# Dealing the last channel block's sums and the meta rows over the token blocks of an output projection

## The chip, the core and the metric

The kernel runs on one core of one Trainium2 chip. The metric is device time in microseconds (us) of the execution, lower is better. Three runs of the kernel before took 1312.33, 1314.13 and 1315.68 us; their median, 1314.13 us, stands for the kernel. The core's engines work side by side, each through its own queue in order: TensorE (PE, matmuls and transposes, with its weight loads as PEld), VectorE (DVE), ScalarE (ACT), GpSimd (POOL) and SyncE (SP), which issues the DMAs.

## The reference

One decoder layer over 1024 tokens of width 1024, with 16 learned meta rows put ahead of them. Cut to what matters here:

```python
a = rmsnorm(h, ln_mix_pre)                       # h: 16 meta rows, then 1024 tokens
proj = a @ w_in
y_diff = diff_attention(...)                     # 512 channels
y_hgrn = hgrn2(...)                              # 512 channels
mix = concatenate([y_diff, y_hgrn], -1) @ w_out  # the output projection, 1024 x 1024
h = h + rmsnorm(mix, ln_mix_post)
a = rmsnorm(h, ln_ffn_pre)
y = conv_ffn(a, ...)                             # 1024 -> 5632, causal convolution of width 3, -> 1024
h = h + rmsnorm(y, ln_ffn_post)
return h[N_META:]
```

The meta rows are dropped at the end, but the convolution looks two rows back, so the last two of them go through the output projection and the norms as well.

## The kernel before

All products are taken in three matmuls of 32-bit operands: each operand is split into a high part and a low part (names ending in `h` and `l`), and high x high, high x low and low x high are added in PSUM.

Tokens are cut into blocks 1 to 8 of 128 rows; "block 0" is the two meta rows. The eight channel blocks k = 0 to 7 of the mixed heads (128 channels each) are stored to DRAM (`msc`) and loaded again per token block: tile `mp` holds channels 0 to 6 or 0 to 7 of a token block, loaded in two halves, and `m7` holds channel block 7 of all eight token blocks. The output projection has two halves of 512 output columns. The first half ran beside the last head; the result of channel blocks 0 to 6 lies in `y0`. Channel block 7 was not ready then, so its product is still to be added: `out_last(p)` does that for token block p. It is three matmuls into a bank `pz`, an addition into `y0` on VectorE, a squared sum on ScalarE (tile `jz`, sums in `ssy`), a small scaling, and for p < 3 the multiplication with the gain on GpSimd (`y0_gain`); later blocks get their gain at the head of their own turn.

The change lies in the loop over i = 1 to 8 of the second half. A turn of it:

- issues the DMAs for the next block: `second_load` (two halves of `mp`, lines L1041) and `load_xh` (the residual rows, L1189);
- runs `run` = `out_part` for k = 0 to 3 into bank `py`, 12 matmuls (lines L1012, L1014, L1016), then `trans(i - 2)`, eight transposes (L1230) of the normalised rows `a` of an earlier block, then k = 4 to 7, 12 more;
- calls `post(i)`: squared sum of the second half on ScalarE (`junk`), `tmp` = sum x gain on VectorE, the reciprocal root from two small ScalarE steps, two VectorE steps that add both halves to the residual `xh`, its store to DRAM (`hsc`, L1210), then the second norm: a square over 1024 columns on ScalarE, two small steps, and the VectorE step that writes `a`.

After `trans` ScalarE copies the transposed rows into `at`. When enough blocks are there, `t_split` casts a quarter of `at` to its high part on ScalarE (`t`) and VectorE takes the low part; the feed-forward matmuls (`pq`) start from them. `meta_part` computes the second half of block 0 with 17 matmuls (L1025 and three of `out_part`), which `post(0)` takes up.

TensorE's order is written out by hand in the program (it is the order of the calls). The other engines' queues are ordered by a scheduler that weighs costs of its own, so a call that is moved also moves rows on VectorE, ScalarE, GpSimd and SyncE. Nearly all their instructions carry line L53, a helper; they are told apart by tile names. The eight PSUM banks (`ps_b`) go round in the order of the calls. The tiles of `mp` share three places: block 2's place was block 7's of the first half, block 4's was block 1's.

The weights `wo` of the second half are loaded and split while the first half ends; the low part of the last of them (`wol`, k = 7) is made on VectorE.

Of the kernel before, what the change touches and what calls it, by code (L numbers as in the profile page):

```python
# [22 lines left out]
KD = D // P  # L23
# [62 lines left out]
def layer_kernel(ctx: ExitStack, tc: tile.TileContext, x, meta, table, lbl, gpre, gpost, win,  # L86
# [76 lines left out]
    def rstd_of(dst, ss, n):  # L163
        A.activation(dst, ss, AF.Ln, bias=eps[: dst.shape[0]], scale=1.0 / n)
        A.activation(dst, dst, AF.Exp, scale=-0.5)
# [3 lines left out]
    def long_tile(name):  # L169
        return mxp.tile([P, 8, WN[0]], F32, tag="X0", name=name).rearrange("p a c -> p (a c)")  # L170
# [833 lines left out]
    def tok(i):  # L1004
        return (2, 14) if i == 0 else (P, start(i))

    def out_part(m, py, wo, ks, first, last):
        r = m.shape[-1]
        for k in ks:
            hi, lo = wo[k]  # L1010
            mh, ml = m[:, 0, k], m[:, 1, k]
            T.matmul(py[:r], mh, hi, start=(first and k == ks[0]), stop=False)  # L1012
            yield 216
            T.matmul(py[:r], mh, lo, start=False, stop=False)  # L1014
            yield 216
            T.matmul(py[:r], ml, hi, start=False, stop=(last and k == ks[-1]))  # L1016
            yield 216
# [42 lines left out]
    def y0_gain(p):  # L1060
        r = tok(p)[0]
        return G.tensor_tensor(y0[:r, p], y0[:r, p], gpo0[:r], op=ALU.mult)

    def out_last(p):
        r = tok(p)[0]
        py = ps_b(f"pz{p}")
        m = m0_7 if p == 0 else k7(p)
        for _ in out_part(m, py, wo0[KD - 1:], range(1), True, True):
            pass
        V.tensor_tensor(y0[:r, p], y0[:r, p], py[:r], op=ALU.add)  # L1070
        junk = qp.tile([P, 512], F32, tag="junk", name=f"jz{p}", bufs=1)
        A.activation(junk[:r], y0[:r, p], AF.Square, accum_out=ssy[:r, p, 0:1])
        A.activation(ssy[:r, p, 0:1], ssy[:r, p, 0:1], AF.Identity, bias=eps[:r], scale=1.0 / D)
        if p < 3:
            y0_gain(p)
# [27 lines left out]
    def ps_b(name):  # L1103
        return pp.tile([P, 512], F32, tag="b", name=name)
# [65 lines left out]
    wo = load_wo(1)  # L1170
# [20 lines left out]
    def post(i, py, free=None):  # L1191
        r, t0 = tok(i)
        xh = xhs.pop(i)
        if i % 2:
            a2 = long_tile(f"a2_{i}")[:, :D]
        elif i == 0:
            a2 = xh
        else:
            a2 = bp.tile([P, D], F32, tag="a2", name=f"a2_{i}", bufs=1)
        tmp = qp.tile([P, 512], F32, tag="tmp", name=f"tmp{i}", bufs=1)  # L1200
        junk = qp.tile([P, 512], F32, tag="junk", name=f"junk{i}", bufs=1)
        s1, s2 = ssy[:r, i, 1:2], ssy[:r, i, 2:3]
        A.activation(junk[:r], py[:r], AF.Square, accum_out=s1)
        V.tensor_tensor(tmp[:r], py[:r], gpo[:r], op=ALU.mult)
        A.activation(s1, s1, AF.Ln, bias=ssy[:r, i, 0:1], scale=1.0 / D)
        A.activation(s1, s1, AF.Exp, scale=-0.5)
        V.scalar_tensor_tensor(xh[:r, :512], y0[:r, i], s1, xh[:r, :512], ALU.mult, ALU.add)
        V.scalar_tensor_tensor(xh[:r, 512:], tmp[:r], s1, xh[:r, 512:], ALU.mult, ALU.add)
        if i:
            SY.dma_start(hsc[P * (i - 1): P * i, :], xh)  # L1210
        if i:
            A.activation(a2[:r], xh[:r], AF.Square, accum_out=s2)
        else:
            s3 = ssy[:r, i, 3:4]
            for half, s_ in ((0, s2), (1, s3)):
                A.activation(free[:r], xh[:r, 512 * half:512 * half + 512], AF.Square, accum_out=s_)
            V.tensor_tensor(s2, s2, s3, op=ALU.add)
        rstd_of(s2, s2, D)
        V.scalar_tensor_tensor(a2[:r], xh[:r], s2, gfb[:r], ALU.mult, ALU.mult)
        a2t[i] = a2  # L1220

    def trans(i):
        r, t0 = tok(i)
        a2 = a2t.pop(i)
        cs = slice(t0 - 14, t0 - 14 + r)
        for half in range(2):
            pt = ps_b(f"pa2_{i}_{half}")
            for j in range(4):
                k = 4 * half + j
                T.transpose(pt[:, j * r:(j + 1) * r], a2[:r, P * k: P * (k + 1)], ident[:r, :r])  # L1230
            pv = pt[:, : 4 * r].rearrange("p (k t) -> p k t", k=4)
            ks = slice(4 * half, 4 * half + 4)
            for p in range(2):
                lo_, hi_ = max(cs.start, C0[p]), min(cs.stop, C0[p] + 2 * WN[p])
                if lo_ < hi_:
                    A.copy(
                        at2[p][:, ks, lo_ - C0[p]:hi_ - C0[p]], pv[:, :, lo_ - cs.start:hi_ - cs.start])
# [32 lines left out]
    def run(*args):  # L1270
        for _ in out_part(*args):
            pass

    def k7(i):
        return m7[:, i - 1:i].rearrange("p b l t -> p l b t")

    for i in range(1, NBLK):
        py = ps_b(f"py1_{i}")
        if i >= 3:
            y0_gain(i)  # L1280
        if i == 1:
            load_xh(1)
            load_xh(0)
        if i + 1 < NBLK:
            second_load(i + 1)
            load_xh(i + 1)
        run(blocks[i], py, wo, range(4), True, False)
        if i == 3:
            trans(1)
        if i > 3:  # L1290
            trans(i - 2)
        if i == 5:
            trans(0)
        run(blocks[i], py, wo, range(4, 7 if i == 1 else 8), False, i > 1)
        if i == 1:
            pm = ps_b("py1_0")
            for _ in meta_part(pm, wo, True):
                pass
            for p in range(3):
                out_last(p)  # L1300
            run(k7(1), py, wo[KD - 1:], range(1), False, True)
            post(1, py)
            ysum = xhs.pop("sum")
            for l in range(2):
                A.copy(ysum[:2, 512 * l:512 * l + 512], pm[32 * l:32 * l + 2])
            G.tensor_tensor(ysum[:2, :512], ysum[:2, :512], ysum[:2, 512:], op=ALU.add)
            for p in (3, 4):
                out_last(p)
            continue
        post(i, py)  # L1310
        if i == 2:
            post(0, ysum[:, :512], ysum[:, 512:])
        if i == 5:
            t_split(0, 0, quarter(0, 0), ep, "e0")
            t_split(0, 4, quarter(0, 4), ep, "e1")
        if i == 7:
            t_split(0, 7, quarter(0, 7), mxp, "X2", WN[0])
            t_split(0, 6, quarter(0, 6), mxp, "X1", WN[0])
        if i in (2, 3):
            for p in (1 + 2 * i, 2 + 2 * i):  # L1320
                out_last(p)
    close(q_cm, ml_cm, y_cm, wo_cm, ws_cm)

    xu_cm, xup = pool("xu", 2)
# [363 lines left out]
```

## Time and profile before

| | |
|---|---|
| median of 3 runs | 1314.13 us (1312.33 to 1315.68) |
| profiled execution, its own time | 1315.74 us |
| its span, first to last instruction | 1313.9 us |
| mean granted TensorE clock | 0.996 |
| TensorE busy | 1283.4 us, 98% |
| VectorE busy | 887.4 us, 68% |
| ScalarE busy | 697.6 us, 53% |
| GpSimd busy | 482.0 us, 37% |

Times in the rows are counted from the span's start. The stage of the change lies between about 556 us (the first matmuls of block 1's second half) and 645 us. A row of the timeline is: start, duration, engine, line, operation, out<-in, shapes, count, and in brackets the idle time of the engine before it and what ended that. In a table of stretches a row is: stretch, its length, busy time and count of PE, PEld, DVE, ACT and POOL, then the granted clock, the busy share of the DMA engines and GB/s. A row of waits is: who waited, for whom, us in total, times, the longest. Matmuls overlap, so the pace is read from starts, not from durations.

### The profile page before, as it was taken

To read this page: it belongs to the slowest core of one execution; us is meant where nothing else is said; L and a number is where in the kernel's file an instruction comes from. 1 tells how busy PE (TensorE), PEld (TensorE's weight loads), DVE (VectorE), ACT (ScalarE), POOL (GpSimd) and SP (SyncE) were. 2 spreads that over 40 slices of the span, in tenths; PEclk is the share of its full clock that TensorE was granted. 3 is DMA by queue.
4 is the path that set the end of the run, shared out by engine and by line. 5 is a ranking of instruction groups with operands and counts; after the bars stand their busy time and mean duration, and the time that the engine had idled before them with its cause. 6 is when DMAs were issued, how large, how long until landed. Compare 5 with 4: busy or idle time off the path is not lost.

```text
span 1313.9 us, 26100 instructions
## 1 busy us (share of the span) xinstructions
PE 1283.4 (98%) x10154; PEld 1188.1 (90%) x10154; DVE 887.4 (68%) x1488; ACT 697.6 (53%) x1639; POOL 482.0 (37%) x387
## 2 busy tenths in 40 slices
PE   8999999999999999999999999999999999999997
PEld 7999999899989998777999999999999997888875
DVE  7574646465645574547897877877778768697586
ACT  8565466547644763456754544444544445464553
POOL 5231423232313310353066566576666631010121
PEclk9999999999999999998999999999999999999999
DMA  6243655273643533687222222222222138854263
GB/s 212 93 102 84 126 113 113 66 149 84 115 120 67 121 109 108 227 274 252 87 73 78 85 75 79 86 76 81 76 79 88 57 104 282 310 194 162 87 209 120
DMA packets 116418, 165.04 MB, mean 126 GB/s; under 512 B 10099, under 2 KB 57523, under 8 KB 116294
## 3 DMA queue, kind: packets, MB, share of 16 engines
q1 hardware_dynamic: 93062, 151.84, 34.9%
q0 software_dynamic: 23232, 11.54, 7.5%
q8 instruction: 80, 1.31, 0.4%
q14 instruction: 44, 0.36, 0.1%
HBM read 134.24 MB, written 52.17 MB: 142 GB/s over the span
## 4 chain that ended last, share of the span: by engine, by line
PE 49%; DVE 4%; ACT 2%; issue 1%; DVEq 0%; ACTq 0%
PE pd L1537 5%; PE pd L1538 5%; PE pd L1536 5%; PE pb L1378 4%; PE pb L1380 4%; PE pb L1379 4%; PE pa L1378 3%; PE pa L1380 3%; PE pa L1379 3%; PE pc L1380 3%; PE pc L1378 3%; PE pc L1379 3%; DVE t L53 1%; DVE c L53 1%; PE py L1012 1%
## 5 line engine op out<-in xcount | busy, mean ns | idle before, releaser
L1378 PE MATMUL pb<-t,uh 128*128 128x258 f32 x504 | 142.4, 283 | 2.3 <-DVE u L53 2.3
L1379 PE MATMUL pb<-t,uh 128*128 128x258 f32 x504 | 141.8, 281 | 0.0
L1380 PE MATMUL pb<-t,ul 128*128 128x258 f32 x504 | 141.8, 281 | 0.0
L1537 PE MATMUL pd<-wl,gh 128*128 128x512 f32 x308 | 122.0, 396 | 1.2 <-DVE wl L53 1.1
L1536 PE MATMUL pd<-wh,gh 128*128 128x512 f32 x308 | 121.7, 395 | 0.0
L1538 PE MATMUL pd<-wh,gl 128*128 128x512 f32 x308 | 121.6, 395 | 0.0
L53 DVE SCALAR_TENSOR_TENSOR c<-uu,cwt,c 128x514 f32<-128x514 f32 (+1 forms) x88 | 96.9, 1101 | 20.0 <-ACT c L53 19.3
L53 POOL TENSOR_TENSOR c<-c,c 128x514 f32<-128x514 f32 (+1 forms) x44 | 63.8, 1450 | 122.5 <-ACT c L53 119.1
L1378 PEld LDWEIGHTS pb<-t,uh 128*128 128x128 f32 x504 | 95.0, 189 | 2.7 <-DVE u L53 2.7
L1380 PEld LDWEIGHTS pb<-t,ul 128*128 128x128 f32 x504 | 95.1, 189 | 0.0
L1378 PE MATMUL pa<-t,uh 128*128 128x258 f32 (+1 forms) x336 | 95.1, 283 | 0.0
L1379 PEld LDWEIGHTS pb<-t,uh 128*128 128x128 f32 x504 | 95.1, 189 | 0.0
L1380 PE MATMUL pc<-t,ul 128*128 128x258 f32 (+1 forms) x336 | 95.0, 283 | 0.0
L1380 PE MATMUL pa<-t,ul 128*128 128x258 f32 (+1 forms) x336 | 94.9, 282 | 0.0
L1378 PE MATMUL pc<-t,uh 128*128 128x258 f32 (+1 forms) x336 | 94.7, 282 | 0.0
L1379 PE MATMUL pa<-t,uh 128*128 128x258 f32 (+1 forms) x336 | 94.6, 282 | 0.0
L1379 PE MATMUL pc<-t,uh 128*128 128x258 f32 (+1 forms) x336 | 94.5, 281 | 0.0
L53 DVE SCALAR_TENSOR_TENSOR c<-ug,cwt,c 128x514 f32<-128x514 f32 (+1 forms) x88 | 88.3, 1005 | 1.3 <-ACT c L53 0.6
L53 ACT CAST uh<-ra 128x512 fp32r<-128x512 f32 x67 | 41.2, 618 | 62.9 <-PE pb L1379 41.4
L53 POOL TENSOR_TENSOR ul<-ws,uh 128x512 fp32r<-128x512 f32 x42 | 59.1, 1408 | 39.3 <-ACT uh L53 39.3
L1537 PEld LDWEIGHTS pd<-wl,gh 128*128 128x128 f32 x308 | 57.7, 187 | 16.6 <-DVE wl L53 2.6
L53 DVE TENSOR_TENSOR ul<-ra,uh 128x512 fp32r<-128x512 f32 x42 | 39.8, 947 | 48.5 <-ACT uh L53 48.5
(388 smaller groups left out, 4176.3 us busy)
## 6 DMA issues: line engine op xcount, KB each, us to landing
ra<-in_wup_dram SPq DMA_DIRECT2D x88, 256.0 KB, 2.7
mp<-msc SPq DMA_DIRECT2D x23, 512.0 KB, 5.5
tsc<-in_wdown_dram SPq DMA_DIRECT2D x44, 256.0 KB, 4.4
wi<-tsc SPq DMA_DIRECT2D x44, 256.0 KB, 2.8
gi<-gsc SPq DMA_DIRECT2D x33, 256.0 KB, 4.7
wi<-in_wdown_dram SPq DMA_DIRECT2D x33, 256.0 KB, 5.2
gsc<-c SPq DMA_DIRECT2D x22, 257.0 KB, 2.1
tsc<-in_wdown_dram POOLq DMA_DIRECT2D x22, 256.0 KB, 7.4
```

The costliest lines, as they stand in the source:

```text
L53: ins = call(*args, **kw)
L1012: T.matmul(py[:r], mh, hi, start=(first and k == ks[0]), stop=False)
L1378: T.matmul(pt, hi[:, s], th[:, k], start=(first and k == 0), stop=False, skip_group_check=True)
L1379: T.matmul(pt, hi[:, s], tl[:, k], start=False, stop=False, skip_group_check=True)
L1380: T.matmul(pt, lo[:, s], th[:, k], start=False, stop=(k == 3), skip_group_check=True)
L1536: T.matmul(py, gh[:, s], wh, start=(k == 0 and pr not in (3, 7)), stop=False, skip_group_check=True)
L1537: T.matmul(py, gh[:, s], wl, start=False, stop=False, skip_group_check=True)
L1538: T.matmul(py, gl[:, s], wh, start=False, stop=(k == NH - 1), skip_group_check=True)
```

## The change

Three things are put elsewhere; nothing is computed that was not computed before.

- The calls of `out_last`, formerly three in turn 1 before block 1's own last matmuls, two after them and two each in turns 2 and 3, follow a table `LASTS`: turn 1: blocks 1 and 2; turn 2: 3; turn 3: 4 and 5; turn 4: 0 and 6; turn 5: 7 and 8. They come ahead of `post(i)`.
- The meta rows' second half (`meta_part`) moves from turn 1 to the end of turn 2, `post(0)` from turn 2 to turn 4, the transposes `trans(0)` from turn 5 to turn 6, and with them the two `t_split` calls that need all early rows.
- The condition on `trans(i - 2)` is written in another way with the same result.

```diff
+    LASTS = {1: (1, 2), 2: (3,), 3: (4, 5), 4: (0, 6), 5: (7, 8)}
+
     for i in range(1, NBLK):
...
         run(blocks[i], py, wo, range(4), True, False)
-        if i == 3:
-            trans(1)
-        if i > 3:
-            trans(i - 2)
-        if i == 5:
+        if i > 2:
+            trans(max(i - 2, 1))
+        if i == 6:
             trans(0)
         run(blocks[i], py, wo, range(4, 7 if i == 1 else 8), False, i > 1)
+        for p in LASTS.get(i, ()):
+            out_last(p)
         if i == 1:
+            run(k7(1), py, wo[KD - 1:], range(1), False, True)
+        post(i, py)
+        if i == 2:
             pm = ps_b("py1_0")
             for _ in meta_part(pm, wo, True):
                 pass
-            for p in range(3):
-                out_last(p)
-            run(k7(1), py, wo[KD - 1:], range(1), False, True)
-            post(1, py)
             ysum = xhs.pop("sum")
...
-            for p in (3, 4):
-                out_last(p)
-            continue
-        post(i, py)
-        if i == 2:
+        if i == 4:
             post(0, ysum[:, :512], ysum[:, 512:])
-        if i == 5:
+        if i == 6:
             t_split(0, 0, quarter(0, 0), ep, "e0")
             t_split(0, 4, quarter(0, 4), ep, "e1")
...
-        if i in (2, 3):
-            for p in (1 + 2 * i, 2 + 2 * i):
-                out_last(p)
```

How this moves rows in the queues, at three places. In the names, `py1_2` is the bank of block 2's second half, `pz3` the one of `out_last(3)`, `woh1_7` the high part of the second half's weights for k = 7 (`woh0_7` the first half's), `mp1_2` block 2's input, `a2_5` block 5's normalised rows, `xh5` its residual rows and `pa2_4` its neighbour block 4's transposes; the last number of a name only counts buffers.

TensorE, between block 1's first 21 matmuls and block 2. Before (first rows of each group of three, and the meta rows' first and last):

```order
L1016 MATMUL py1_1_7064<-woh1_6_7041,mp1_1_6928 128x512
L1025 MATMUL py1_0_7095<-woh1_0_7005,m0_86 34x512
...
L1014 MATMUL py1_0_7095<-wol1_7_7048,m0_7_88 2x512
...
L1025 MATMUL py1_0_7095<-woh1_6_7041,m0_86 34x512
L1012 MATMUL pz0_7113<-woh0_7_6322,m0_7_88 2x512
...
L1012 MATMUL pz1_7122<-woh0_7_6322,m7_7051 128x512
...
L1012 MATMUL py1_1_7064<-woh1_7_7047,m7_7051 128x512
...
L1012 MATMUL pz4_7168<-woh0_7_6322,m7_7051 128x512
...
L1012 MATMUL py1_2_7176<-woh1_0_7005,mp1_2_7069 128x512
```

And now:

```order
L1016 MATMUL py1_1_7064<-woh1_6_7041,mp1_1_6928 128x512
L1012 MATMUL pz1_7095<-woh0_7_6322,m7_7051 128x512
L1014 MATMUL pz1_7095<-wol0_7_6323,m7_7051 128x512
L1016 MATMUL pz1_7095<-woh0_7_6322,m7_7051 128x512
L1012 MATMUL pz2_7104<-woh0_7_6322,m7_7051 128x512
L1014 MATMUL pz2_7104<-wol0_7_6323,m7_7051 128x512
L1016 MATMUL pz2_7104<-woh0_7_6322,m7_7051 128x512
L1012 MATMUL py1_1_7064<-woh1_7_7047,m7_7051 128x512
L1014 MATMUL py1_1_7064<-wol1_7_7048,m7_7051 128x512
L1016 MATMUL py1_1_7064<-woh1_7_7047,m7_7051 128x512
L1012 MATMUL py1_2_7130<-woh1_0_7005,mp1_2_7069 128x512
```

Of 35 matmuls between the two blocks nine are left; the meta rows' 17 stand behind block 2, and three sums stand further back.

ScalarE, around block 5's square (`a2_5`), which the transposes of block 7's turn wait for. Before:

```order
L53 COPY t0_0_7449<-at2_0_6975 128x1032
L53 COPY t0_4_7452<-at2_0_6975 128x1032
L53 ACTIVATE junk5_7437,ssy_6270<-py1_5_7380 128x512
L53 ACTIVATE ssy_6270<-ssy_6270 128x1 x2
L53 COPY at2_0_6975<-pa2_4_0_7474 128x4x128
L53 COPY at2_0_6975<-pa2_4_1_7480 128x4x128
L53 ACTIVATE a2_5_7435,ssy_6270<-xh5_7328 128x1024
```

And now:

```order
L53 ACTIVATE junk5_7425,ssy_6270<-py1_5_7364 128x512
L53 COPY at2_0_6975<-pa2_4_0_7456 128x4x128
L53 ACTIVATE ssy_6270<-ssy_6270 128x1
L53 COPY at2_0_6975<-pa2_4_1_7462 128x4x128
L53 ACTIVATE ssy_6270<-ssy_6270 128x1
L53 COPY at2_0_6975<-pa2_0_0_7468 128x4x2
L53 COPY at2_0_6975<-pa2_0_1_7474 128x4x2
L53 COPY t0_0_7506<-at2_0_6975 128x1032
L53 COPY t0_4_7509<-at2_0_6975 128x1032
L53 ACTIVATE a2_5_7423,ssy_6270<-xh5_7281 128x1024
L53 ACTIVATE junk6_7494,ssy_6270<-py1_6_7437 128x512
```

The two casts `t0_0` and `t0_4` stood ahead of block 5's own rows by a whole turn; now they, and the meta row's copies, stand between block 4's copies and block 5's square. VectorE's rows moved in the same way: its low parts of `t0_0` and `t0_4`, and block 6's `tmp`, now come ahead of block 5's `a2_5`.

SyncE, from block 2's load on. Before:

```order
L1041 DMA mp1_2_7069<-msc_92 128x2x512 x2
L1189 DMA xh2_7072<-in_x_dram 128x1024
L1041 DMA mp1_3_7177<-msc_92 128x2x512 x2
L1041 DMA mp1_4_7252<-msc_92 128x2x512 x2
L1125 DMA ra2_22_7989<-in_wup_dram 128x512
L1125 DMA ra2_21_7991<-in_wup_dram 128x512
L1210 DMA hsc_89<-xh1_7065 128x1024
```

And now:

```order
L1041 DMA mp1_2_7069<-msc_92 128x2x512 x2
L1189 DMA xh2_7072<-in_x_dram 128x1024
L1041 DMA mp1_3_7131<-msc_92 128x2x512 x2
L1210 DMA hsc_89<-xh1_7065 128x1024
L1041 DMA mp1_4_7205<-msc_92 128x2x512 x2
```

Up to block 3's load the queue is the same; block 4's load moved behind the store of block 1's rows, and the two weight loads `ra2` moved further back.

## The prediction

> **What bounds the kernel now.** I read the head of the page first, then the table of waits on TensorE in the stage of the change (555 to 690 us), then the same stretch in the order of time, and last the DMA landings and the chain of waits.
>
> ```profile
> span 1313.9 us, 26100 instructions
> PE 1283.4 (98%) x10154; PEld 1188.1 (90%) x10154; DVE 887.4 (68%) x1488; ACT 697.6 (53%) x1639; POOL 482.0 (37%) x387
> PE pa L1230 <- DVE a L53: 3.3, 1, 3.3
> PE pb L1378 <- DVE u L53: 2.3, 2, 1.4
> PE py L1014 <- DVE wol L53: 1.1, 1, 1.1
> ```
>
> TensorE is busy for 98% of the span, so a change of order can only win what TensorE waits for, or what its clock loses. In this stage the waits are 1.1 us for the last weight split, 3.3 us for block 3's normalised rows `a` (the transposes of L1230 in block 5), and 2.3 us of later waits that the change does not touch.
>
> The clock belongs to the 3.3 us wait:
>
> ```profile
> 607.47:609.60 2.13, 0.00 (x0) 0.00 (x0) 0.85 (x1) 2.13 (x10) 1.27 (x1) 1.00 1.05 328
> 609.61:610.73 1.12, 0.00 (x1) 0.01 (x1) 1.12 (x2) 0.65 (x4) 0.00 (x0) 0.50 0.62 229
> 610.73:616.43 5.70, 5.70 (x23) 4.78 (x24) 3.24 (x5) 3.80 (x10) 0.00 (x0) 0.50 0.71 214
> 616.43:623.00 6.57, 6.57 (x34) 5.47 (x33) 4.24 (x5) 3.72 (x8) 0.00 (x0) 1.00 0.87 282
> ```
>
> The third number from the right is the granted clock. 2.13 us into the wait it falls to 0.50 and stays there for 6.82 us, 5.70 of them after work resumed. Half speed over 5.70 us loses 2.85 us, so this one wait costs 3.26 + 2.85 = 6.1 us. It is the largest sum in the stage.
>
> **The change, part by part.** The clock of TensorE's program around the change:
>
> ```profile
> 573.36 0.40 PE L1016 MATMUL py<-woh,mp 128*128 128x512 f32 x1
> 573.59 0.40 PE L1025 MATMUL py<-woh,m 128*34 128x512 f32 x1
> 575.74 0.40 PE L1014 MATMUL py<-wol,m 128*2 128x512 f32 x1 [1.14 <-DVE wol L53]
> 583.17 0.40 PE L1012 MATMUL py<-woh,mp 128*128 128x512 f32 x1
> 588.77 0.39 PE L1012 MATMUL pz<-woh,m 128*128 128x512 f32 x1
> 607.07 0.40 PE L1016 MATMUL py<-woh,mp 128*128 128x512 f32 x1
> 610.73 1.97 PE L1230 MATMUL pa<-ident,a 128*128 128x128 f32 x8 [3.26 <-DVE a L53]
> 620.69 0.87 PE pa L1230 x8
> ```
>
> Block 2's 24 matmuls run from 583.17 to 588.77, which is 0.233 us each (the 0.39 of a row overlaps the next). Eight transposes take 0.87 us. A block with its transposes is 6.5 us.
>
> *Removed ahead of block 2.* The 17 meta matmuls and the eighth-channel sums of meta, 3 and 4 (9 matmuls) leave the place between 573.59 and 583.17: 26 x 0.233 = 6.05 us. They come back later in the same number, so TensorE's work is unchanged; block 2 may only start earlier. What is left ahead of it is nine matmuls: two sums, 1.4 us, to 574.99, then block 1's own eighth-channel group, whose second matmul needs the same split that ended the 1.14 us wait at 575.74. It ends at 575.74 + 2 x 0.233 = 576.2.
>
> *What is late next: block 2's input.* Its tile `mp` is loaded in two halves. The landing of each stands here, first half, then second:
>
> ```profile
> L1041 SPq DMA_DIRECT2D mp<-msc x1: 530/530/530, 573.5 to 573.5; - x1
> DMA to landing us min/median/max: 8.1/8.1/8.1
> L1041 SPq DMA_DIRECT2D mp<-msc x1: 1161/1161/1161, 574.1 to 574.1; - x1
> DMA to landing us min/median/max: 8.9/8.9/8.9
> 574.00:583.20 9.20, 8.06 (x35) 4.61 (x35) 7.19 (x7) 5.09 (x13) 7.25 (x6) 1.00 0.99 347
> ```
>
> 573.5 + 8.1 = 581.6, and 574.1 + 8.9 = 583.0. Before, block 2 came at 583.17 and the loads hid behind the meta rows. Nothing that SP issues ahead of these loads is moved, and the DMA engines are 0.99 busy with what was queued before, so I take 581.6 unchanged. TensorE then idles from 576.2 to 581.6, 5.4 us. Block 2 starts 1.5 us earlier than before and owes 6.05 us: +4.5 us. Block 3's halves were issued right after (576.2 onward) and are not wanted before 594. Block 4's load now stands behind the store of block 1's rows on SP; it is wanted only at 602, and I cost it at nothing.
>
> *The clock after that idle time.* No row shows 5.4 us of idle. The nearest is the 3.26 us one. If the half-clock stretch again begins 2.1 us into the idle time and lasts 6.8 us, it ends at 585.1, which is 3.5 us after resumption and loses 1.75 us; if it again outlasts resumption by 5.7 us, it loses 2.85 us. A gain is excluded, as the one longer wait of the stage lost clock. I take the middle, 2.3 us, and keep 1.75 and 2.85.
> The Trainium skill, page "TensorE: Matmul & The Clock Gate", section "What's actually happening", says that the clock falls to half after an idle window of about 3.4 us, recovers after a busy window of that length, and that the windows run freely. By that rule resumption is followed by 3.4 to 6.8 us at half clock, an estimate of 1.7 to 3.4 us lost, and the sum below would end between 1318.3 and 1320.0. Its section "Why this matters for your kernels" asks for no idle gaps over about 3 us, which speaks against this change: it makes one of 5.4 us. The trace agrees on the half clock (0.50) and on its length (6.82 us is two such windows), but fell after 2.13 us of idle time, sooner than the rule says.
>
> *The wait at 610.73 goes.* The new clock of the program: block 2 from 581.6 to 589.5 (5.6 + 2.3), its sum and the meta rows (20 matmuls, 4.7 us) to 594.2, block 3 to 600.7, two sums to 602.1, block 4 to 608.6, two sums to 610.0, and block 5's transposes, which need `a` of block 3, at 612.8. What `a` needs is costed from these rows:
>
> ```profile
> 606.49 1.06 ACT L53 ACTIVATE a<-xh 128x1024 f32<-128x1024 f32 x1 [1.89 <-DVE xh L53]
> 607.54 0.61 ACT L53 ACTIVATE jz<-y 128x512 f32<-128x512 f32 x1
> 618.66 0.53 ACT L53 ACTIVATE ssy<-ssy 128x1 f32<-128x1 f32 x2
> 621.16 1.08 ACT L53 COPY at<-pa 128x512 f32<-128x512 f32 x2 [1.97 <-PE pa L1230]
> 615.11 2.02 ACT L53 CAST t<-at 128x1032 fp32r<-128x1032 f32 x2
> 608.75 1.93 DVE L53 SCALAR_TENSOR_TENSOR a<-xh,ssy,gfb 128x1024 f32<-128x1024 f32 x1 [1.70 <-ACT ssy L53]
> 616.26 2.37 DVE L53 TENSOR_TENSOR t<-at,t 128x1032 fp32r<-128x1032 f32 x2
> ```
>
> ScalarE's queue now puts the copies of block 2's transposes (done at 605.8, copied by 606.9) ahead of the square for `a`: 606.9 + 1.06 and 0.53 for the two small steps is 608.5, and 1.93 on VectorE gives 610.4. That is 2.4 us ahead of 612.8. Gone: 3.26 of wait and 2.85 of clock, -6.1 us. The meta work that filled VectorE and ScalarE between 594 and 603 has moved two blocks on, which is where it is paid.
>
> *New waits in blocks 6 and 7.* Rows for the meta row's steps and for what delays VectorE:
>
> ```profile
> 602.74 1.27 DVE L53 SCALAR_TENSOR_TENSOR xh<-xh,ssy,gfb 2x1024 f32<-2x1024 f32 x1 [0.43 <-ACT ssy L53]
> 612.63 1.01 PE L1230 MATMUL pa<-ident,xh 2*128 2x2 f32 x8
> 585.70 2.81 DVE L53 SCALAR_TENSOR_TENSOR xh<-y,ssy,xh 128x512 f32<-128x512 f32 x1 [0.76 <-ACT ssy L53]
> 588.43 0.74 DVE L53 SCALAR_TENSOR_TENSOR xh<-tmp,ssy,xh 128x512 f32<-128x512 f32 x1
> 581.66 6.29 POOL L53 TENSOR_TENSOR y<-y,gpo 2x512 f32<-2x512 f32 x5
> 608.33 1.27 POOL L53 TENSOR_TENSOR y<-y,gpo 128x512 f32<-128x512 f32 x1 [3.08 <-ACT jz L53]
> ```
>
> Block 6 starts at 610.0 + 6.5 + 1.4 = 617.9; its eight transposes of block 4 run from 620.7 to 621.6, and the meta row's eight small ones, 1.01 us at half clock and so 0.5, to 622.1. Block 7's transposes of block 5 are due at 617.9 + 6.5 + 0.5 + 2.8 = 627.7. In the new order ScalarE first copies both transposes (to 623.2), then does the two casts `t` (2.02, to 625.2), block 5's square (1.06), block 6's square (0.61) and the small steps (0.53, to 627.4), and only then can VectorE make `a` (1.27), at 628.7: 1.0 us of new wait that nothing hides.
>
> The meta row's own `a` is due at 621.6. ScalarE copies block 5's transposes by 614.8 and scales the meta row by 615.2; three VectorE steps of 0.7 end at 617.2, the squares ahead in ScalarE's queue at 618.2, block 7's (0.61 and its small step, 0.9) at 619.1, small steps 0.53, `a` 1.27: 620.9, or 0.7 us early, if GpSimd stays out of the way. It may not: the same VectorE step takes 0.74 us alone and 2.81 us while GpSimd's gains run, and the 1.93 us `a` at 608.75 lies on the gain at 608.33. The gains of blocks 7 and 8 (1.27 each) now come right there. Two collisions less 0.7 of slack give 1.8 us, so this wait is 0 to 1.8; one collision more, at block 4's rows, is allowed for with 0.9. New waits: 1.0 to 3.7 us, taken at 2.5, a little over the middle, as every gain in the rows above met a VectorE step. Each stays under 2.13 us, so I charge no clock for them.
>
> *The rest of the way.* What the shift of block 8 does to the end is read here:
>
> ```profile
> 643.47 1.28 DVE L53 SCALAR_TENSOR_TENSOR a<-xh,ssy,gfb 128x1024 f32<-128x1024 f32 x1 [1.45 <-ACT ssy L53]
> 644.59 0.96 ACT t L53
> 646.71 1.22 DVE t L53
> 650.00:660.00 10.00, 10.00 (x86) 10.00 (x85) 10.00 (x10) 7.59 (x12) 0.00 (x0) 1.00 0.01 2
> ```
>
> VectorE's last `a` waits for ScalarE, that one for TensorE's block 8; behind it VectorE is busy without a break (10.00 of 10.00). No slack is left that would swallow a shift: it passes to the end one for one. The feed-forward stage has the same instructions as before.
>
> **The sum.** +4.5 (start of block 2 and work owed) + 2.3 (clock) - 6.1 (old wait and its clock) + 2.5 (new waits) = +3.2 us. The profiled execution took 1315.7 us (span 1313.9 and 1.8 around it, which the change leaves alone), 1.6 above the median of 1314.13; runs lie from 1312.33 to 1315.68. Part of that spread may be the old half-clock stretch itself, which a run can be spared; a run without it has less to win too, so the new time is not lowered by it. Forecast: 1318.9 us, 0.36% above the median. About 0.3% (3.9 us: 1310.2 to 1318.1) is what a measurement can tell from no change.
>
> **The rivals.**
> *The load is in time.* If block 2's first half landed by 576.2, 8.1 us would shrink to 2.7, there would be no 5.4 us of idle time and no half clock: 1318.9 - 5.4 - 2.3 = 1311.2, and 1309.7 with the new waits at their floor. It decides at a landing of about 577.7, where the saving on the old wait is still whole and the idle time too short for the clock to fall. Against it stands the 0.99 DMA share; for it, only that fewer transfers are queued behind.
> *The new waits stay at their floor*, with the short half-clock stretch: 4.5 + 1.75 - 6.1 + 1.0 = +1.15, 1316.9 us, no difference that can be told. For it speaks that GpSimd has only two gains left there.
> *A second half-clock stretch.* The waits in blocks 6 and 7 add up inside a few us, and 2.13 us sufficed once: +2.85, 1321.8 us.
> *The old wait stays.* If GpSimd's two sums of feed-forward weights fall on block 3's `a`, it comes 2 to 3 us later than 610.4 and the wait returns in part, up to its 6.1: up to 1325.0 us. The change would then not do what it moves work for.
>
> **How the numbers follow.** Likeliest, the sum: 0.44, with a range of its own from 1317.5 to 1321. Floor of the new waits: 0.28. Load in time: 0.12, of which 0.08 below 1310.2 and 0.04 above. Second stretch: 0.09. Old wait stays: 0.07. Slower 0.44 + 0.09 + 0.07 = 0.60; same 0.28 + 0.04 = 0.32; faster 0.08. The range from 1314.5 to 1323 leaves out the load in time and the upper end of the last case; its lower end is the floor case less the 1.6 us by which the profiled execution stands over the median, and a little.
>
> **What would show it.** In the changed kernel's profile: a wait of TensorE of about 5.4 us before block 2's first matmul, ended by the DMA of `mp`, with a granted clock of 0.50 behind it; no wait at block 5's transposes; a wait near 1 us at block 7's transposes and up to 1.8 at the meta transposes. The forecast is wrong if the first is under 2 us, if block 5's wait is still there, or if the clock falls again between 615 and 635.

## The result, and the profile after

The changed kernel took 1318.5 us (median of nine runs, 1316.62 to 1322.23) against 1314.13 us (median of nine, 1312.33 to 1318.39) for the kernel before. The ratio is 1.0031, with a 95% interval of 1.0017 to 1.0045: slower by 0.2 to 0.5%, with the forecast at 1318.9. Its profiled execution took 1317.35 us.

The head of the page of the changed kernel, and its table of waits on TensorE between 555 and 700 us:

```profile
span 1315.5 us, 26099 instructions
PE 1283.0 (98%) x10154; PEld 1187.7 (90%) x10154; DVE 884.1 (67%) x1488; ACT 697.3 (53%) x1639; POOL 480.6 (37%) x387
PE py L1012 <- DMA mp<-msc: 4.9, 1, 4.9
PE pb L1372 <- DVE u L53: 2.3, 2, 1.4
PE pa L1230 <- DVE xh L53: 1.4, 1, 1.4
PE pa L1230 <- DVE a L53: 0.9, 1, 0.9
PE ss L574 <- DVE on L53: 0.6, 1, 0.6
PE py L1014 <- DVE wol L53: 0.2, 1, 0.2
```

The busy times stand as before; what moved is the waiting. The old 3.3 us for `a` in block 5 is gone, and so is most of the 1.1 us for `wol`. In their place stand 4.9 us for block 2's `mp`, 1.4 us for the meta row (`xh`) in block 6 and 0.9 us for `a` in block 7. The waits for `u` (2.3 us) and for `on` (0.4 us before, 0.6 now, at 557 to 558 us) lie behind and ahead of the change and are left out of the sums below. The rows of the timeline, of TensorE, VectorE and GpSimd, and the load in the chain of waits:

```profile
580.46 0.79 PE L1012 MATMUL py<-woh,mp 128*128 128x512 f32 x1 [4.91 <-DMA mp<-msc]
620.89 0.65 PE L1230 MATMUL pa<-ident,xh 2*128 2x2 f32 x8 [1.36 <-DVE xh L53]
628.17 1.09 PE L1230 MATMUL pa<-ident,a 128*128 128x128 f32 x8 [0.85 <-DVE a L53]
...
606.57 1.68 DVE L53 SCALAR_TENSOR_TENSOR a<-xh,ssy,gfb 128x1024 f32<-128x1024 f32 x1 [1.78 <-ACT ssy L53]
617.73 1.23 DVE L53 TENSOR_TENSOR ssy<-ssy 2x1 f32<-2x1 f32 x1
...
617.50 1.44 POOL L53 TENSOR_TENSOR y<-y,gpo 128x512 f32<-128x512 f32 x1 [5.30 <-ACT jz L53]
...
573.13 7.29 DMA mp<-msc
```

Block 2 starts when its load lands, 7.3 us after the issue. Block 3's `a` is done at 608.25, 2.4 us before block 5's transposes. The addition of two numbers for the meta row takes 1.23 us beside a gain of GpSimd. The table of stretches around the hole (third number from the right: granted clock):

```profile
575.54:579.94 4.40, 0.01 (x1) 0.00 (x0) 3.64 (x4) 1.78 (x5) 2.42 (x3) 1.00 0.99 366
579.95:580.46 0.51, 0.00 (x0) 0.00 (x0) 0.00 (x0) 0.48 (x3) 0.51 (x1) 0.50 1.09 434
580.46:583.36 2.90, 2.90 (x7) 2.32 (x8) 2.01 (x3) 1.35 (x5) 1.59 (x2) 0.50 1.03 399
583.36:587.00 3.64, 3.64 (x18) 2.92 (x16) 1.30 (x2) 1.65 (x4) 0.00 (x0) 1.00 0.95 308
```

The clock fell 4.4 us into the idle time and came back 2.9 us after work resumed: a loss of 2.9 / 2 = 1.45 us.

Before, the stage had 3.3 + 1.1 us of these waits and 2.85 us of clock, 7.25 us in all. After, it has 4.9 + 1.4 + 0.9 + 0.2 and 1.45, 8.85 us. The difference of 1.6 us is that of the two profiled executions (1317.35 - 1315.74), but that it fits to the tenth is chance. The length of the stage, from the start of block 1's first matmul in it to the start of block 8's last, can be read for both; first before, then after:

```profile
568.70 0.40 PE L1012 MATMUL py<-woh,mp 128*128 128x512 f32 x1
637.15 0.39 PE L1016 MATMUL py<-woh,mp 128*128 128x512 f32 x1
...
567.67 0.40 PE L1012 MATMUL py<-woh,mp 128*128 128x512 f32 x1
638.14 0.39 PE L1016 MATMUL py<-woh,mp 128*128 128x512 f32 x1
```

That is 68.45 and 70.47 us, so the stage itself took 2.0 us longer. It began 1.0 us earlier, and 0.6 us more were lost behind it.

The medians lie 4.4 us apart: the profiled execution of before stood 1.6 us above its median, that of the changed kernel 1.15 us below. Part of what differs between executions of one program is the granted clock: its mean went from 0.992 (1319.7 and 1322.2 us) to 0.997 (1317.4 and 1318.0 us) in the nine runs of the changed kernel.

### The profile page after: what moved, and what is told of

It is laid out like the page before. It is cut to its first block, busy times and chain, and to the rows that moved or that the text cites. A ratio compares the mean times of both kernels' runs of the same rounds, so it can differ in the third digit from the quotient of the medians.

```text
span 1315.5 us, 26099 instructions
## 1 busy us (share of the span) xinstructions
PE 1283.0 (98%) x10154; PEld 1187.7 (90%) x10154; DVE 884.1 (67%) x1488; ACT 697.3 (53%) x1639; POOL 480.6 (37%) x387
## 4 chain that ended last, share of the span: by engine, by line
PE 85%; DVE 5%; ACT 4%; issue 2%; DMA 2%; POOL 0%; DVEq 0%; SPq 0%; ACTq 0%; POOLq 0%
PE pd L1531 5%; PE pd L1532 5%; PE pd L1530 5%; PE pb L1372 4%; PE pb L1374 4%; PE pb L1373 4%; PE pa L1372 3%; PE pa L1374 3%; PE pa L1373 3%; PE pc L1374 3%; PE pc L1372 3%; PE pc L1373 3%; PE pa L732 3%; PE py L1016 1%; PE py L1012 1%
```

## The experiments

Theory A: the load of block 2 comes too late for the shortened turn 1; the hole before block 2 is the price, in time and in clock, and the late tail of the meta rows is the gain. Theory B: the new waits in blocks 6 and 7 set the pace, so that time won earlier is given back there. All were compared with the kernel before on the same chip, whose median in these comparisons lay between 1314.46 and 1314.98 us. Tables of waits show only the rows that the text uses.

**The hole filled with the meta rows' matmuls.**

```diff
-        if i == 2:
+        if i == 1:
             pm = ps_b("py1_0")
             for _ in meta_part(pm, wo, True):
```

> Changed kernel, but the meta rows' 17 matmuls are put back into turn 1, right ahead of block 2; the deal of the sums, post(0) in turn 4 and trans(0) in turn 6 stay as changed. Theory A (block 2's late load is the price, and the idle time before it costs clock too): the 17 matmuls take 17 x 0.233 = 4.0 us of the 4.9 us hole, about 0.9 us is left, too short for the clock to fall, and all of it passes to the end: 1318.5 - 4.0 - 1.4 to 2.9 = 1311.6 to 1313.1 us, and the clock reads 1.00 from 575 to 600. Theory B (the new waits at the transposes of blocks 6 and 7 set the pace, so idle time taken away earlier comes back there): those waits grow from 2.2 to 5 us or more and the time stays at 1317 to 1319 us.

Measured: 1313.81 us, ratio to before 0.9998 (0.9990 to 1.0007); 4.7 us under the changed kernel. Its waits:

```profile
PE pa L1230 <- DVE xh L53: 1.9, 1, 1.9
PE py L1012 <- DMA mp<-msc: 1.4, 1, 1.4
PE pa L1230 <- DVE a L53: 0.7, 1, 0.7
```

The wait for `mp` shrank by 3.5 us and no half clock followed it, as theory A says. But the wait for the meta row grew from 1.4 to 1.9 us, and this time a half-clock stretch of 3.41 us came behind it, at 618.8: 1.7 us that theory A had not counted. It ended 0.7 us above the range. Theory B has the lesser part: some was given back, most was not.

**The load issued earlier.**

```diff
+    second_load(2)
     gfb = qp.tile([P, D], F32, tag="gfb", name="gfb", bufs=1)
...
-            second_load(i + 1)
+            if i > 1:
+                second_load(i + 1)
```

> Changed kernel, but the two halves of block 2's mp are issued ahead of the loads of gfb and xh of block 1 (1 MB, about 3 us at the 347 GB/s of the stage) and not behind them. Theory A: the first half lands about 3 us earlier, near 577.4, the wait before block 2 falls from 4.9 to about 1.9 us, under the 2.13 us after which the clock fell before: 1318.5 - 3.0 - 1.4 to 2.9 = 1312.6 to 1314.1 us. Rival (the landing is set by the whole queue of transfers, not by the two ahead of it): it lands near 580 as before and the time stays at 1317 to 1319. Theory B (later waits take it back): wait shorter, time unchanged.

Measured: 1315.86 us, ratio 1.0003 (0.9990 to 1.0016); its profiled execution took 1313.77. The timeline of TensorE at block 2:

```profile
576.65 0.50 PE L1012 MATMUL py<-woh,mp 128*128 128x512 f32 x1 [1.09 <-DMA mp<-msc]
```

The two transfers ahead were what made the load late: block 2 starts 3.8 us earlier, after a wait of 1.1 instead of 4.9 us. The load was issued 2.1 us earlier (571.02 instead of 573.13 us) and landed 5.6 instead of 7.3 us after that. The profiled execution is where theory A put it, the median 2 us higher. In this kernel too the wait for the meta row was 1.9 us, followed by 3.41 us at half clock, and its runs spread from 1312.5 to 1318.9.

**The hole filled with work that nobody needs.**

```diff
+            fill = ps_b("fill")
+            for n in range(6):
+                run(k7(1), fill, wo[KD - 1:], range(1), n == 0, n == 5)
         post(i, py)
```

> Changed kernel with 18 more matmuls (128x512) into a bank of their own, read by nobody, between block 1's last matmul and block 2: work that is not needed, which fills 4.2 us of the 4.9 us hole. The landing of mp is not moved, so the wait itself is still paid; only the clock can be saved. Theory A: no half-clock stretch behind it, 1318.5 - 1.4 to 2.9 = 1315.6 to 1317.1 us. Rival (the half clock there costs nothing, because block 2's second half and later loads set the pace): 1318 to 1319 us.

Measured: 1316.98 us, ratio 1.0023 (1.0014 to 1.0032), 1.5 us under the changed kernel, with no half clock in the stage:

```profile
574.50:579.00 4.50, 4.50 (x20) 3.45 (x19) 4.16 (x4) 1.36 (x4) 2.55 (x2) 1.00 1.01 381
579.00:585.00 6.00, 6.00 (x26) 4.78 (x26) 2.39 (x4) 3.91 (x12) 2.54 (x2) 1.00 0.93 346
```

The medians alone do not settle it: by their ratios to the kernel before, the two kernels lie 1.0 us apart, and the intervals overlap. The profiles do. From the start of block 2 to the start of block 8's last matmul, without the waits in between, this one took 54.25 us (579.15 to 636.18, less 2.8), the changed kernel's 55.5 (580.46 to 638.14, less 2.2): 1.2 us more, for 1.45 us of clock worked out above. A second execution of the changed kernel (below) took 56.8 us, 2.55 more, for 2.9 us of clock. So the half clock behind the hole does cost time.

**Only the tail of the meta rows moved, from the kernel before.**

```diff
-        if i == 5:
+        if i == 6:
             trans(0)
...
-        if i == 2:
+        if i == 4:
             post(0, ysum[:, :512], ysum[:, 512:])
-        if i == 5:
+        if i == 6:
             t_split(0, 0, quarter(0, 0), ep, "e0")
```

> Kernel before, with only the meta rows' tail moved: post(0) from turn 2 to turn 4, trans(0) and the first two t_split from turn 5 to turn 6. The meta rows' matmuls and the deal of the sums stay as before. Theory A (the meta rows' steps on VectorE and ScalarE made block 3's a late): the 3.3 us wait before block 5's transposes and its 2.9 us of clock go, no hole before block 2 comes, the new waits at the transposes of blocks 6 and 7 (2.2 us in the changed kernel) come: 1314.1 - 6.1 + 2.2 = 1310.2 us, 1309 to 1312. Rival (the sums of 5 to 8, two a turn in turns 2 and 3, made it late): the wait at block 5's transposes stays and the time is 1314 us or more.

Measured: 1312.67 us, ratio 0.9980 (0.9972 to 0.9989): faster. The waits, and the meta row's addition on VectorE:

```profile
PE py L1012 <- DMA mp<-msc: 1.5, 1, 1.5
PE py L1014 <- DVE wol L53: 0.7, 1, 0.7
PE py L1012 <- ACT woh L53: 0.4, 1, 0.4
PE pa L1230 <- DVE xh L53: 0.3, 1, 0.3
...
612.71 0.14 DVE L53 TENSOR_TENSOR ssy<-ssy 2x1 f32<-2x1 f32 x1
```

The wait for `a` and its half clock are gone, so the tail alone is the gain of the change. It was 0.7 us outside the range expected, because a wait nobody had on the list came: 1.5 us for block 7's `mp`. Its place is that of block 5, so its load can only be issued when block 5 is done, one block ahead of its use; the first half was issued at 611.12 and landed at 620.1. With no gain of GpSimd beside it the meta row's addition took 0.14 us.

**Only the sums dealt, and only the meta rows' matmuls moved.** First the sums; the calls that the table replaces are taken out.

```diff
+    LASTS = {2: (3,), 3: (4, 5), 4: (6,), 5: (7, 8)}
...
+        for p in LASTS.get(i, ()):
+            out_last(p)
```

> Kernel before, with only the sums dealt over the turns (3 in turn 2; 4 and 5 in turn 3; 6 in turn 4; 7 and 8 in turn 5; 0 to 2 stay in turn 1). All that belongs to the meta rows stays as before. Theory A (the meta rows' steps on VectorE and ScalarE in turn 2 made the 3.3 us wait before block 5's transposes, as moving them alone took it away): that wait stays at 2.5 to 3.5 us with the half clock behind it, a load wait of 0 to 1.2 us before block 2 is added, 1314 to 1316 us. Theory S (VectorE was simply full there, and taking two or three sums of 0.67 us away does as well): the wait falls to about 1.3 us, no half clock, 1314.5 - 2.0 - 2.9 = 1309.6 to 1312 us.

Measured: 1314.86 us, ratio 0.9998 (0.9989 to 1.0008).

```profile
PE pa L1230 <- DVE a L53: 4.2, 3, 2.2
PE py L1012 <- DMA mp<-msc: 0.2, 1, 0.2
...
599.77 0.98 PE L1230 MATMUL pa<-ident,a 128*128 128x128 f32 x6 [2.21 <-DVE a L53]
609.91 0.77 PE L1230 MATMUL pa<-ident,a 128*128 128x128 f32 x5 [1.18 <-DVE a L53]
```

The time is theory A's, the picture is neither's: the wait at block 5 fell to 1.2 us, as theory S says, but 2.2 us came up at block 4 and 0.8 at block 7. Dealing the sums spreads the old wait, and gains nothing.

Then the meta rows' matmuls; the same lines are taken out of turn 1.

```diff
         if i == 2:
+            pm = ps_b("py1_0")
+            for _ in meta_part(pm, wo, True):
+                pass
...
             post(0, ysum[:, :512], ysum[:, 512:])
```

> Kernel before, with only the meta rows' 17 matmuls moved from turn 1 to the end of turn 2, right ahead of post(0); the deal of the sums, post(0) in turn 2 and trans(0) in turn 5 stay as before. Theory A (the matmuls taken out of turn 1 leave a hole in which the load of mp is late): block 2 would be due 4.0 us earlier, at about 579, the load lands near 581, so a wait for mp of 1.4 to 2.5 us, with up to 1.7 us of half clock; the wait for a before block 5 stays or grows, since the meta rows' steps come later than before: 1314.7 + 1.4 to 4.2 = 1316 to 1319 us. Rival (only the hole of 4.9 us, which the sums dealt away make as long as that, costs something): 1314.7 us.

Measured: 1316.56 us, ratio 1.0014 (1.0005 to 1.0023), inside theory A's range: a wait for `mp` and the old wait at block 5 side by side. Its stretches around both:

```profile
576.88:580.26 3.38, 0.00 (x0) 0.00 (x0) 3.38 (x5) 1.58 (x5) 1.41 (x2) 1.00 1.04 391
580.26:587.00 6.74, 6.74 (x29) 4.98 (x30) 4.54 (x5) 4.22 (x16) 5.93 (x5) 1.00 0.78 296
608.60:611.14 2.54, 0.00 (x1) 0.00 (x1) 1.93 (x1) 2.54 (x10) 2.40 (x2) 1.00 0.16 61
611.14:612.80 1.66, 1.66 (x17) 1.48 (x17) 1.31 (x3) 0.82 (x4) 1.07 (x1) 1.00 0.42 57
612.81:616.22 3.41, 3.41 (x9) 2.71 (x9) 0.95 (x3) 2.68 (x9) 0.00 (x0) 0.50 0.95 261
```

The 3.38 us hole cost no clock at all, while 2.54 us of idle time later did. How long TensorE idles does not decide alone.

**The meta row's transposes later; three edits at once; another deal.**

```diff
-        if i == 6:
-            trans(0)
         run(blocks[i], py, wo, range(4, 7 if i == 1 else 8), False, i > 1)
+        if i == 6:
+            trans(0)
```

> Changed kernel, with the meta rows' transposes, trans(0), put behind block 6's last matmuls instead of between k = 3 and k = 4: 12 matmuls or 2.8 us later. It takes away the wait of 1.4 us for the meta row's xh (1.4 to 1.9 us in the runs so far). Theory A: 1318.5 - 1.4 = 1317.1 us, to 1315.4 where a half-clock stretch of 3.4 us went with it; the 4.9 us wait before block 2 stays. Rival (the two casts t, which need the meta rows, come later too, and block 5's a behind them): the wait at block 7's transposes grows from 0.9 to 2 us or more and the time stays at 1318 to 1319.

Measured: 1317.09 us, ratio 1.0014 (1.0005 to 1.0023): the 1.4 us of theory A in the median. The profiled execution took 1317.46 us, no less than the changed kernel's 1317.35. The rival was at work in part: the wait at block 7's transposes grew from 0.9 to 1.4 us, and a later wait for `u`, 2.3 us in most kernels, grew to 3.3.

> Changed kernel with three edits at once: meta rows' matmuls in turn 1, block 2's load ahead of gfb and xh, trans(0) behind block 6's last matmuls. If the waits add up as theory A has it, then against the kernel with the first edit alone (1313.8 us, waits of 1.4 us for mp and 1.9 us for xh, 3.4 us at half clock): 1313.8 - 1.4 - 1.9 - 1.7 = 1308.8 us, to 1310.5 where the half clock was only in some of its runs. If a later wait takes the gain back (block 7's load of mp, or block 5's a behind the casts): 1312 to 1314 us.

Measured: 1312.82 us, ratio 0.9985 (0.9975 to 0.9995). No wait for `mp` and none for the meta row are left, but this, in its stretches:

```profile
611.54:613.49 1.95, 0.01 (x1) 0.00 (x0) 1.95 (x4) 1.77 (x7) 0.36 (x1) 1.00 0.92 259
613.49:614.31 0.82, 0.82 (x7) 0.82 (x8) 0.82 (x1) 0.00 (x0) 0.82 (x1) 1.00 0.97 355
614.31:617.72 3.41, 3.41 (x11) 2.73 (x10) 2.84 (x4) 2.96 (x10) 1.86 (x2) 0.50 0.70 262
```

Block 4's `a` is 1.95 us late for block 6, and 3.41 us at half clock follow: 3.65 us given back. Here theory B had it. Once the hole is gone, the rows of VectorE and ScalarE around the meta row's tail are the next to be late. Here too the later wait for `u` was 3.3 us.

```diff
-    LASTS = {1: (1, 2), 2: (3,), 3: (4, 5), 4: (0, 6), 5: (7, 8)}
+    LASTS = {1: (1, 2, 3, 4), 2: (5,), 3: (6,), 5: (7, 8)}
```

> The three edits together with another deal: sums 1 to 4 in turn 1 ahead of block 1's own group, the meta rows and their sum behind it, 5 in turn 2, 6 in turn 3, 7 and 8 in turn 5. Against the kernel before with only post(0) late (1312.7 us): its waits of 1.1 us for the last weights (hidden by the sums ahead), 1.5 us for block 7's mp (the sums of turn 5 lie between) and 0.3 us for xh go: 1309.8 us, 1308.5 to 1311. If GpSimd's gains of 7 and 8, which lengthen VectorE's steps, fall on block 4's and 5's rows again: 1 to 2 us more.

Measured: 1314.15 us, ratio 0.9993 (0.9984 to 1.0001), 4.3 us above what was expected. `a` came late three times (3.3 us in all), and there were two stretches of 3.41 us at half clock, one of them at 671.8, behind a wait of 2.2 us for `u`. The load waits were gone as expected; why `a` was late three times was not taken apart.

**The tail late, and an order of turn 1 that hides both loads.** From the kernel with only the tail moved:

```diff
+            for p in (1, 2):
+                out_last(p)
+            run(k7(1), py, wo[KD - 1:], range(1), False, True)
+            post(1, py)
             pm = ps_b("py1_0")
             for _ in meta_part(pm, wo, True):
                 pass
-            for p in range(3):
-                out_last(p)
-            run(k7(1), py, wo[KD - 1:], range(1), False, True)
-            post(1, py)
+            out_last(0)
...
-        if i in (2, 3):
-            for p in (1 + 2 * i, 2 + 2 * i):
-                out_last(p)
+        for p in {2: (5, 6), 3: (7,), 5: (8,)}.get(i, ()):
+            out_last(p)
```

> Kernel before, with the meta rows' tail late (post(0) in turn 4, trans(0) and the first two t_split in turn 6), in turn 1 the sums of 1 and 2, block 1's own group and post(1) ahead of the meta rows' matmuls, and the sums 5 and 6 in turn 2, 7 in turn 3, 8 in turn 5. Against the kernel with only the tail late (1312.7 us): the wait of 1.1 us for the last weights is hidden by the sums, and 0.7 of the 1.5 us wait for block 7's mp by the sum of block 8: 1310.9 us, 1310 to 1312. If a gain of GpSimd falls on the meta rows' steps, a wait of 1 to 2 us at their transposes comes back, with up to 1.7 us of half clock: 1312 to 1314.5 us.

Measured: 1309.29 us (1308.63 to 1310.26), ratio 0.9962 (0.9948 to 0.9975). It beats both kernels, by 5 and by 9 us. Beside the 2.3 us for `u`, its waits in the stage are

```profile
PE py L1012 <- DMA mp<-msc: 0.6, 1, 0.6
PE py L1014 <- DVE wol L53: 0.4, 1, 0.4
...
609.17 0.14 DVE L53 TENSOR_TENSOR ssy<-ssy 2x1 f32<-2x1 f32 x1
```

and no half clock in the stage. It ended 0.7 us below the range: against the kernel with only the tail late, the waits fell by 1.9 us, as expected, and the profiled time by 3.5. Of the other 1.6 us, 0.8 lie ahead of the stage, which began at 567.62 instead of 568.40, and 0.2 behind it; 0.6 us stand in no wait.

**The changed kernel once more.**

> The changed kernel once more, unedited, for its time beside the others and for the clock behind the hole before block 2 in another execution. Theory A with the clock going by whole stretches of 3.41 us: again a wait of about 5 us for mp, behind it 0.50 that ends 3 to 6 us after work resumed, by where in the idle time the stretch began; 1318.5 us, 1317 to 1320 as median. Rival (the 2.9 us of half clock after resumption is a fixed time): it ends 2.9 us after resumption again.

Measured: 1318.71 us, ratio 1.0034 (1.0022 to 1.0047). The stretches around its 4.7 us hole:

```profile
576.10:579.81 3.71, 0.00 (x0) 0.00 (x0) 3.58 (x4) 1.13 (x2) 2.02 (x2) 1.00 0.97 344
579.82:580.79 0.97, 0.00 (x0) 0.00 (x1) 0.04 (x1) 0.94 (x5) 0.69 (x1) 0.50 1.09 427
580.79:586.64 5.85, 5.85 (x14) 4.61 (x15) 2.96 (x4) 3.19 (x11) 1.82 (x2) 0.50 0.99 362
```

Same program, same hole, and 5.85 us of half clock behind it instead of 2.90: 2.9 us lost instead of 1.45. The stretch is 6.83 us long, twice the 3.41 us of the first profile. This execution's waits (7.0 us) and clock (2.9) are 2.65 us over those of before, its time 2.97.

**The meta row's collision with GpSimd.**

```diff
-    LASTS = {1: (1, 2), 2: (3,), 3: (4, 5), 4: (0, 6), 5: (7, 8)}
+    LASTS = {1: (1, 2), 2: (3,), 3: (4, 5), 4: (0, 6), 6: (7, 8)}
```

> Changed kernel, with the sums of blocks 7 and 8 in turn 6 instead of turn 5, so that their gains on GpSimd and their additions on VectorE come behind the meta rows' last steps. Theory A (a gain of GpSimd lengthened the meta row's 2x1 addition from 0.14 to 1.23 us, and the additions stood ahead of it): that addition takes 0.14 us; VectorE's queue ahead of the meta row's a is 1.1 + 2 x 0.67 = 2.4 us shorter, TensorE comes 6 x 0.233 = 1.4 us earlier, so the wait of 1.4 us for xh falls to about 0.4 us: 1318.7 - 1.0 = 1317.7 us, to 1316.5. Rival (ScalarE's order of squares sets the meta row's time): the wait grows to 2 us or more, 1318.5 to 1321 us.

Measured: 1320.4 us, ratio 1.0050 (1.0037 to 1.0064). A miss of 2.7 us; the time is in the rival's range, but not for the rival's reason, as the wait for `xh` did not grow. Its waits and the addition:

```profile
PE pa L1230 <- DVE a L53: 2.7, 1, 2.7
PE pa L1230 <- DVE ssy L53: 1.3, 1, 1.3
PE pa L1230 <- DVE xh L53: 0.8, 1, 0.8
...
617.66 0.14 DVE L53 TENSOR_TENSOR ssy<-ssy 2x1 f32<-2x1 f32 x1
```

The collision was what was said: without the gain the addition takes 0.14 us, and the wait for `xh` falls from 1.4 to 0.8 us. But TensorE came 1.4 us earlier without the sums, and block 4's `a` did not, which makes the wait of 1.3 us (the table names `ssy`, the step that follows that `a` on VectorE); a half-clock stretch of 3.41 us followed, and block 6's `a` came 2.7 us late for block 8. Both were left out of the expectation. Waits of 10.2 us are the most of any kernel here, and the time is the longest.

**The sum of all.** Waits of the stage (without those for `u` and `on`) and clock lost in it (half of the half-clock time in which TensorE worked) of each profile, against the length of the stage and the time:

| kernel | median us | waits | clock | both, against before | stage, against before | profiled time, against before |
|---|---|---|---|---|---|---|
| before | 1314.13 | 4.4 | 2.85 | 0 | 0 (68.45) | 0 (1315.74) |
| changed | 1318.5 | 7.4 | 1.45 | +1.6 | +2.0 | +1.6 |
| changed, again | 1318.71 | 7.0 | 2.9 | +2.65 | +2.7 | +3.0 |
| meta matmuls back in turn 1 | 1313.81 | 4.4 | 1.7 | -1.15 | -0.9 | -2.2 |
| load earlier | 1315.86 | 3.4 | 1.7 | -2.15 | -1.7 | -2.0 |
| hole filled (4.2 us of matmuls counted as wait) | 1316.98 | 7.4 | 0 | +0.15 | +0.5 | -0.6 |
| tail only | 1312.67 | 2.9 | 0 | -4.35 | -3.6 | -3.6 |
| meta matmuls only | 1316.56 | 5.9 | 1.7 | +0.35 | +0.3 | -0.7 |
| sums only | 1314.86 | 5.6 | 1.7 | +0.05 | +0.7 | -1.0 |
| meta row's transposes later | 1317.09 | 6.9 | 2.6 | +2.25 | +2.4 | +1.7 |
| three edits | 1312.82 | 2.5 | 1.7 | -3.05 | -2.7 | -3.4 |
| another deal | 1314.15 | 3.3 | 1.7 | -2.25 | -1.5 | -1.1 |
| tail and order | 1309.29 | 1.0 | 0 | -6.25 | -6.2 | -7.1 |
| sums later | 1320.4 | 10.2 | 3.1 | +6.05 | +6.3 | +4.7 |

Waits and clock give the length of the stage within 0.8 us for every kernel. The profiled times lie up to 1.7 us off the stage, mostly because the stage began 0.3 to 2.1 us later in the profile of before than in the others.

The parts alone cost -2, +2 and 0 us in the medians (each against its own comparison); together +4. They do not add. By waits and clock of the profiles the parts sum to -3.95 us, the whole is +1.6. Of the 5.55 us between, 3.75 are clock: each part alone lost less than the 2.85 us of before (0, 1.7 and 1.7), a saving that can be had only once. Another 1.7 us are waits at the transposes. The sums dealt away also made the hole 1.5 us longer (4.9 against 3.4) than the meta rows' matmuls alone did.

## Why the prediction was right, point by point

- *Block 2's load is late next* (5.4 us, +4.5): right. 4.9 and 4.7 us in two executions; with the `wol` wait down from 1.1 to 0.2 it is +4.0. The load landed 7.3 instead of 8.1 us after its issue. The rival that it lands in time fell by 2.7 us (580.4 for the 577.7 it needed). The kernel with the earlier load comes near it: 1315.86 us in the median, no gain over before, and 1313.77 in the profile, where the wait for the meta row and its half clock took the place of the hole. Neither is the 1311.2 us that was worked out.
- *The clock after that idle time* (2.3 us, 1.75 to 2.85): right in size on average, wrong in how it was built. The two executions lost 1.45 and 2.9 us, each just outside the bounds, 2.2 in the mean; two other kernels with the same hole lost 1.4 and 2.6. There is no fixed delay of 2.1 us and no fixed length of 6.8 us to carry over from the old wait: half clock comes in stretches of 3.41 us, one or two of them.
- *The old wait goes* (-6.1 us): right to the tenth, and by the mechanism told: block 3's `a` was 2.4 us ahead, as worked out. The experiments name the part: the late tail of the meta rows, not the deal of the sums.
- *New waits* (2.5 us, 1.0 to 3.7): right in sum, 1.4 + 0.9 = 2.3 us, and 1.0 + 0.9 in the second execution. For the meta row this is partly luck. Of the two collisions counted one came, the addition of 1.23 instead of 0.14 us; the second gain started at 620.40 and the meta row's `a`, from 619.56, took its usual 1.27. And the 0.7 us of slack was not there: by these rows, without the 1.09 us the row would have been done at 619.74, 0.2 us after TensorE was due at 619.53. The two errors nearly cancel. The third collision, at block 4's rows, did not come.
- *"I charge no clock for them"*: true of the two profiles, but not a safe step. Waits of 1.9 us, under the 2.13 us that it rested on, drew a half-clock stretch in four of the kernels above.
- *The shift passes to the end one for one*: right. From the stage's first matmul to the last matmul of the kernel the changed kernel took 2.65 us longer, of which the stage has 2.0, and 3.4 with 2.7 in the second execution; for the kernel with the longest stage it is 6.5 with 6.3, for the fastest -6.0 with -6.2. Where the later wait for `u` or its clock grew (meta row's transposes later, three edits, another deal), 1.0 to 1.8 us more were lost behind the stage.
- *The sum* (+3.2): +1.6 and +3.0 in the two profiles, +4.4 between the medians. The start was 1315.74 us, a run 1.6 us above the median of its kernel. So that the forecast of 1318.9 lies 0.4 us from the measured 1318.5 is partly luck: its steps are not that exact.

## What to carry to other kernels

Work moved out of a turn also uncovers the load behind it: compare the new due time with the landing in the trace of before, and move the load, or leave work there that needs nothing late. Test the parts of such a change apart; here one part gained 0.2%, one lost 0.1% and one did nothing, and only the gain, with an order that hides the loads, gave 0.4%. After each gain look for the next row that is late by a microsecond, as the old profile does not show it.

## What the runs showed of the hardware that was not expected

Half clock came in whole stretches: of the 13 between 570 and 680 us, over the profiles of all kernels, ten lasted 3.41 us and three 6.83. The full-clock stretches before and between them fit the same grid: each of the 27 in the clock records of the fourteen traces is a whole number of 3.4133 us to within 0.01 us, such as 566.61 (166 of them), 597.33 (175) and 37.55 (11). Call one unit of this grid a window. The window before each fall held 1.59 to 3.41 us of idle time; other windows of the stage with up to 1.64 us, and two with 1.76 and 1.80, were not followed by a fall, so no sharp limit can be read from them. So a hole of 3.38 us that fell half into one window and half into the next (1.80 and 1.58 us) cost no clock, and one of 1.95 us inside one window did. That is read off the idle times and the clock records; no run shifted the windows on purpose. It also shows why the same hole cost 1.45 us of clock once and 2.9 the other time: how long half clock stays goes by the window that it fills. A half-clock window with up to 0.58 us of idle time was followed by full clock (0.51 in the first execution of the changed kernel), the three with 0.97 (its second execution), 1.12 and 1.70 us by another window at half clock. The Trainium skill, page "TensorE: Matmul & The Clock Gate", section "What's actually happening", gives windows of 3413 ns that run freely, and the length agrees with the 3.41 us here; it lets the clock fall after an idle window, where about half a window sufficed here (1.59 us at the least).

The spread of the runs goes with this only in part. Two kernels without a stretch in their profiles and with small waits lay close (tail only: eleven runs within 2.6 us; tail and order: five within 1.6), while the kernel before, in the same two comparisons, spread over 7.4 us (33 runs) and 4.3 us (15 runs), with a mean granted clock from 0.994 to 0.998 in the former. But the eleven runs of the kernel with the meta row's transposes later lay within 2.3 us, with a hole of 5.1 us and a stretch of 6.83 in its profile, and those of the kernel with the filled hole, without a stretch, spread over 4.1.

A VectorE addition of 2 x 1 numbers took 0.14 us alone and 1.23 us beside a gain of GpSimd. The Trainium skill, page "SBUF — State Buffer", section "SBUF: two separate sides", says that the two share a port pair as an exclusive lock, held for a whole instruction; the 1.09 us more agrees with that: the addition, from 617.73, ends at 618.96 and the gain, from 617.50, at 618.94.
